# A dilated-attention layer whose weighted sums are queued as filler between the next pair's scores

## The chip, the core and the metric

The kernel runs on one core of a Trainium2 chip. The time is the device time of one execution in microseconds. Matrix products run on TensorE (PE in the profile), elementwise work on VectorE (DVE) and ScalarE (ACT); SyncE (SP) issues the DMAs, and each engine works through its own instructions in a fixed order, waiting on semaphores for the others. What is compared is the median of several executions.

## The reference

A trunk of two layers over 512 tokens of width 1024: layer 0 is a stick-breaking attention, layer 1 the dilated attention that changes here; a feed-forward block and a gated per-layer input follow each. The dilated layer, cut to what matters:

```python
DIL_CONFIGS = ((128, 1), (512, 4), (2048, 16))       # window, dilation; 8 heads of 64 each
def dilated_attention(x, w_in, w_out, cos, sin):
    proj = (x @ w_in).reshape(B, S, G, 3, H, HEAD_DIM)
    for g, (window, dil) in enumerate(DIL_CONFIGS):
        q = apply_partial_rope(proj[:, :, g, 0], cos, sin)
        k = apply_partial_rope(proj[:, :, g, 1], cos, sin)
        v = proj[:, :, g, 2]
        # tokens with the same index modulo dil form a sequence; each attends to a band in it
        o, lse = banded_attention(strided(q), strided(k), strided(v), window // dil)
        ...
    alpha = jax.nn.softmax(jnp.stack(lses, axis=0), axis=0)
    o = jnp.einsum('gbsh,gbshd->bshd', alpha, jnp.stack(outs, axis=0))
    return o.reshape(B, S, H * HEAD_DIM) @ w_out
```

The three groups' softmaxes, weighted by their sums, are one softmax over all keys of the three groups, which is how the kernel computes it.

## The kernel before

Every product is made of three fp32r matmuls (high times high, high times low, low times high), so each operand is split into a rounded part and a rest: ScalarE writes the first (`whi`, `th`, `uh`, `od0h`), VectorE the second (`wlo`, `tl`, `ul`, `od0l`). Weights arrive by DMA and are split the same way in front of their use.

The eight heads are worked through in four pairs. For a pair and a group, `queries(pr, g)` makes the rotated q and k (48 matmuls of 128x512, in two halves), whose outcome VectorE and ScalarE turn into the tiles `dl<pair><group>qa`, `ka`, `la` and so on. `scores` multiplies them (8 matmuls a head) and masks them with a running maximum. `maxima` combines the maxima over groups by transposes, `exps` takes 16 exponentials on ScalarE, in place in the tiles `S`. The sums of a pair are eight steps: `turn` transposes up to four blocks of S on TensorE and splits the result into `th` and `tl`; `apply` multiplies these with the values V (6 or 12 matmuls). Three turns run ahead of the first apply. After four steps of a head, numerators and denominators are combined (`s`, `num`, `den`), and when both heads are through, four reciprocals and a product give the pair's output, split into `od<pair>h` and `od<pair>l`. `out` multiplies these with the output weights, with one step per pair.

Values come first. Those of groups 1 and 2 for the first heads use the normalized input in its order; those of group 0 use copies sorted the other way, `uh` and `ul` (`unsorted`). `sq.columns` and `sq.row` make the row and column factors of the normalization by one-column matmuls; the column factor scales the values, the row factor the rope tables `cs` and `ss`, which every query unit needs.

The order of the work around this is set by a `Filler`: a queue of generators that stands for matmul work with a clock in estimated microseconds. `fill(t)` issues work from the queue for t of its clock, `fill.until(x)` issues until x is done. `due(name)` gives the evacuations on VectorE and ScalarE a place in the order by a due time from the table `TUNE`. In the kernel before, the queue holds all twelve query units and then the second half of the values (`values(1, g)`). The sums are driven from outside: `attend` runs through the steps of one pair (pairs 0 and 1), or of pairs 2 and 3 at once, and calls `tick` after each, which issues queued work and, when a query unit is old enough, the scores of one head (`piece`).

Of the kernel before, what the change touches and what calls it, by code (L numbers as in the profile page):

```python
# [19 lines left out]
P = 128  # L20
T = 512
D = 1024
KT = 8
DFF = 4096
EPS = 1e-6
TUNE = dict(late=4, gap2=1.0, hik=1, lok=0, sqk=1, pieces=4, of=5, og=4, warm=9, wprep=0, s1a=-400, s1b=200, e=25,
            oev=25, qev=-400, hsplit=-200, vev=50, rope=-800, ttr=-100, exps=200, turn=-50, maxi=-50, comb=-100,
            norm=400, res=-400, resk=2, yev=-50, fev=25, gate=0, fin=-50, fe=2.0, ff=0.0, fg=5.0, qlag=5.0, fa=0.57,
            fb=0.32, slope=0.05, lag=8.0, gap=1.2, m0=6.0, m1=5.5, m2=8.0, p0=5.0, p1=2.0, p2=8.0, hp0=6, hp1=30,
            hps=2, blag=1.5, vlag=0.0, fx=5.5, ahead=3, pgap=0.0, vev1=50)  # L30
# [133 lines left out]
def program(tc, ctx, w_dram, x_dram, xs_dram, p_dram, pos_dram, g_dram, c_dram, out_dram):  # L164
# [479 lines left out]
    def dilated(xh, xl, sq, oh, ol, partial, out, prepare):  # L644
        swap = list(range(8, 16)) + list(range(8)) + list(range(16, 32))
        with tc.tile_pool(name="dlw", bufs=1, reuse_waits="tile") as wp:
# [51 lines left out]
                            value_part(g, t0 + 1, ps)  # L698
                        yield 0.72

            def queries(pr, g):
                f = {}

                def evac(m, ps, cs):
                    c, s = norm["rope"]
                    a, b, d = tmp("ra"), tmp("rb"), tmp("rf" + str(m))
                    with due("rope"):
                        dve.stream_shuffle(b, ps, swap)
                        if g:
                            dve.tensor_mul(a, ps, c)  # L710
                            dve.tensor_mul(d, b, s)
                        else:
                            dve.tensor_tensor(sigma(a), cut(ps), cut(c), ALU.mult)
                            dve.tensor_tensor(sigma(d), cut(b), cut(s), ALU.mult)
                        dve.tensor_add(d, d, a)
                    f[m] = d
                    if m == 1:
                        qk[pr, g] = heads_split(f[0], f[1], f"dl{pr}{g}", False, True)

                base = g * 1536 + pr * P  # L720
                yield from linear("w_in_dil", [base, base + 512], xh, xl, evac, bank)

            def scores(S, M, g, h, q, k, kl):

# [58 lines left out]
            def turn(S, order, h, j2):  # L783
# [3 lines left out]
                for j in (2 * j2, 2 * j2 + 1):  # L787
# [6 lines left out]
                    for part in parts:  # L794
                        pe.transpose(ps[:, n:n + P], part, ident)
                        n += P
                fill.clock += 0.45
                th = wp.tile([P, T], F32R, name="th", tag="th", bufs=3)
                tl = wp.tile([P, T], F32R, name="tl", tag="tl", bufs=3)
                with due("turn"):  # L800
# [4 lines left out]
            def apply(pr, order, h, j2, th, tl, out):  # L805
                at = 0
                for j in (2 * j2, 2 * j2 + 1):
                    if order == 0:
                        jobs = [(0, 2 * P if j < 3 else P)]
                    else:  # L810
                        jobs = [(1, P), (2, P)]
                    for g, width in jobs:
                        v = V[g, j]
                        vs, vp = slice(64 * h, 64 * h + P), pr % 2 if g else pr
                        mm3(out[:, j * P:j * P + width], v[:, 0, vp, vs], v[:, 1, vp, vs],
                            th[:, at:at + width], tl[:, at:at + width], j == 0 and g < 2, True)
                        at += width
                fill.clock += 1.3

            def attend(prs, gap, between=None):  # L820
                jobs = [(pr, order, h, j2) for pr in prs for h in range(2) for order in range(2) for j2 in range(2)]
                outs, sums = {}, {}
                ahead = TUNE["ahead"]
                ready, later = [], []
                for j in jobs[:ahead]:
                    ready.append(turn(SS[j[0]], *j[1:]))
                    tick(gap)
                if between is not None:
                    between()

                def divide(pr, num, den):
                    for c in range(4):
                        cs = slice(c * P, (c + 1) * P)
                        i = dve.reciprocal(den[:, cs], den[:, cs])
                        if c == 3:
                            dve.tensor_mul(num, num, den)
                            oh[pr], ol[pr] = split(num, f"od{pr}")
                            later.clear()
                        yield i

                for n, (pr, order, h, j2) in enumerate(jobs):
                    if j2 == 0:
                        outs[order] = wide()
                    apply(pr, order, h, j2, *ready.pop(0), outs[order])
                    if n + ahead < len(jobs):
                        j = jobs[n + ahead]
                        ready.append(turn(SS[j[0]], *j[1:]))
                    if later:
                        after(next(later[0]), norm["turned"])
                    if order == 1 and j2 == 1:  # L850
                        if h == 0:
                            sums[pr] = tmp("num"), tmp("den")
                        num, den = sums[pr]
                        s1 = tmp("s1")
                        hs, ds = HALF[h], HALF[1 - h]
                        with due("comb"):
# [1 line left out]
                            for dst, src in ((den[hs], ds), (num[hs], hs)):  # L858
                                dve.tensor_tensor(cut(dst), sigma(outs[0][src]), cut(s1[src]), ALU.add)
                        if h == 1:  # L860
                            later.append(divide(pr, num, den))
                    tick(gap)
                for d in list(later):
                    run(d)

            vps = {g: [wide(), wide()] for g in (1, 2)}
            for k in range(KT):
                for g in (1, 2):
                    w = W.take("w_in_dil", k, g * 1536 + 1024, 256)
                    for t in range(4):  # L870
                        value_step((xh[k], xl[k]), vps[g][t // 2][:, (t % 2) * 256:(t % 2) * 256 + 256], k, t, *w,
                                   t % 2 == 0)
                if k == 6:
                    norm["col"] = sq.columns(natural_too=True)
                if k == 7:
                    row = sq.row()
            xu = [unsorted(k) for k in range(KT)]
            for g in (1, 2):
                for t in range(4):
                    value_part(g, t, vps[g][t // 2])  # L880
            vps = [bank(), bank(), wide(), wide()]
            for k in range(KT):
                w = W.take("w_in_dil", k, 1024, 512)
                for t in range(4):
# [1 line left out]
            for t in range(4):  # L886
                value_part(0, t, vps[t])
            del xu
            cos, sin = rope_tables()
            rope = [U(n) for n in ("cs", "ss")]  # L890
            dve.tensor_mul(rope[0], cos, row)
            dve.tensor_mul(rope[1], sin, row)
            norm["rope"] = rope
            ones_and_zeros()
            fill = Filler()
            for pr in range(4):
                for g in range(3):
                    fill.add((pr, g), queries(pr, g))
            for g in (1, 2):
                fill.add(("v", g), values(1, g))  # L900
            SS, MM = {}, {}
            pieces = [(pr, g, h) for pr in range(4) for g in range(3) for h in range(2)]

            def piece():
                pr, g, h = pieces.pop(0)
                if pr not in SS:
                    SS[pr], MM[pr] = {}, sp.tile([P, 3, 4, 2], F32, name="M")
                if g < 2:
                    for i2 in range(2):
                        SS[pr][h, g, i2] = U("S")  # L910
                scores(SS[pr], MM[pr], g, h, *(qk.pop((pr, g)) if h else qk[pr, g]))
                fill.clock += 0.87

            def tick(t):
                fill(t)
                if pieces and fill.done.get(pieces[0][:2], 1e9) + TUNE["lag"] <= fill.clock:
                    piece()

            for pr in range(4):
                while pieces and pieces[0][0] == pr:  # L920
                    fill.until(pieces[0][:2], TUNE["lag"])
                    piece()
                    fill(TUNE["pgap"])
                fill(TUNE["m0"])
                N = maxima(MM[pr])
                late = exps(SS[pr], N)[TUNE["late"]:]
                fill(TUNE["m2"])
                if pr < 2:
                    attend([pr], TUNE["gap"])

            def between():
                fill.until(("v", 2))
                for e in late:
                    after(e, norm["last"])
                partial.update({m: bank("out") for m in range(2)})
                fill.add("out", out(partial, (0, 1), range(2)))
                prepare()

            attend([2, 3], TUNE["gap2"], between)
            fill.until("out")  # L940


    def layer(i, h, xh, xl, sq, last):
# [54 lines left out]
        with tc.tile_pool(name=f"ffn{i}", bufs=1, reuse_waits="tile") as fp:  # L998
# [6 lines left out]
            W.pieces = TUNE["pieces"]  # L1005
            if i == 1:
                outs.update({m: wide() for m in range(2, ahead)})
                run(out(outs, range(2, ahead), range(nk - 2)))
                run(out(outs, range(ahead), (nk - 2, nk - 1)))
            run(linear(name, [m * P for m in range(ahead, KT)], oh, ol, lambda m, *a: evac_y(m + ahead, *a),  # L1010
                       banks=wide if i else some(2, bank, wide), nk=nk, halves=True))

# [185 lines left out]
```

## Time and profile before

| quantity | value |
|---|---|
| median of 3 runs | 1470.85 us (1468.16 to 1471.59) |
| profiled execution | 1468.4 us, span 1466.3 us |
| mean granted clock of TensorE | 0.988 |
| TensorE, weight loads | 97%, 82% of the span |
| VectorE, ScalarE, GpSimd | 63%, 47%, 4% |
| the chain that ended last | TensorE 82%, VectorE 10%, ScalarE 5%, issue 2%, DMA 1% |
| the dilated layer up to its output | from 694.2 to 1035.8 us |

The profile is of one execution. Busy time is what an engine spends in its instructions; matmuls are pipelined, and the distance from one start to the next is what one costs in a dense run. In rows of the timeline, square brackets hold the idle time ahead of the instruction and what released it.

### The profile page before, as it was taken

What the parts mean: (1) busy time and instruction counts of PE and PEld (TensorE: products, weight loads), DVE (VectorE), ACT (ScalarE), POOL (GpSimd) and SP (SyncE); (2) the same over time, 40 slices, a digit from 0 to 9 for tenths busy, and PEclk for the clock granted to TensorE, in tenths of its full rate; (3) what the DMA queues carried; (4) which work ended last, traced back from release to release, by engine and by line L of the source; (5) the groups of instructions that cost most, each with busy time, mean ns of one, the idle gap of its engine ahead of it and who ended that gap; (6) DMA issues with size and microseconds to landing.
All of it is one profiled execution on the core that took longest, in us unless ns stands there. A gap on an engine that the chain in (4) does not pass through costs nothing.

```text
span 1466.3 us, 18372 instructions
## 1 busy us (share of the span) xinstructions
PE 1418.8 (97%) x7154; PEld 1198.0 (82%) x7154; DVE 929.6 (63%) x1563; ACT 684.3 (47%) x1042; POOL 56.9 (4%) x33
## 2 busy tenths in 40 slices
PE   9999999999999999999899999898999999999998
PEld 7888888888888888878778787798888888888887
DVE  5888885683353534568759898966783353534476
ACT  4788986543221322355535646644633222222353
POOL 1111110000000000001200000000000000000000
PEclk9999999999999999999899999999999999999999
DMA  5444342333333333223322211220432333333321
GB/s 200 118 113 122 111 117 77 125 96 101 92 96 101 91 97 100 87 87 122 101 64 80 72 46 56 69 70 21 144 98 89 101 93 94 101 89 98 101 74 71
DMA packets 45127, 138.80 MB, mean 95 GB/s; under 512 B 5680, under 2 KB 6448, under 8 KB 45040
## 3 DMA queue, kind: packets, MB, share of 16 engines
q1 hardware_dynamic: 44960, 137.36, 31.5%
q8 instruction: 56, 0.92, 0.3%
q0 software_dynamic: 80, 0.26, 0.1%
q14 instruction: 31, 0.25, 0.1%
HBM read 123.45 MB, written 4.19 MB: 87 GB/s over the span
## 4 chain that ended last, share of the span: by engine, by line
PE 82%; DVE 10%; ACT 5%; issue 2%; DMA 1%; SPq 0%; ACTq 0%; DVEq 0%
PE wb L356 17%; PE wb L358 16%; PE wb L360 16%; PE mmb L356 4%; PE mmb L360 4%; PE mmb L358 3%; DVE wlo L99 2%; PE wb L258 1%; PE wb L259 1%; PE wb L257 1%; ACT S L779 1%; PE mmb L423 1%; PE mmb L425 1%; PE mmb L424 1%; ACT whi L98 1%
## 5 line engine op out<-in xcount | busy, mean ns | idle before, releaser
L98 ACT ACTIVATE whi<-wraw_t 128x1024 fp32r<-128x1024 f32 (+1 forms) x298 | 228.9, 798 | 453.9 <-PE wb L360 345.6
L99 DVE TENSOR_TENSOR wlo<-wraw_t,whi 128x1024 fp32r<-128x1024 f32 (+1 forms) x310 | 276.1, 911 | 234.2 <-ACT whi L98 231.0
L356 PE MATMUL wb<-nh,whi 128*128 128x512 f32 (+1 forms) x594 | 227.3, 385 | 4.4 <-ACT nh L262 4.4
L358 PE MATMUL wb<-nh,wlo 128*128 128x512 f32 (+1 forms) x594 | 226.4, 384 | 0.0
L360 PE MATMUL wb<-nl,whi 128*128 128x512 f32 x576 | 207.6, 391 | 0.4 <-DVE nl L266 0.4
L356 PE MATMUL wb<-fh,whi 128*128 128x512 f32 x496 | 196.5, 396 | 0.0
L360 PE MATMUL wb<-fl,whi 128*128 128x512 f32 x496 | 196.5, 396 | 0.0
L358 PE MATMUL wb<-fh,wlo 128*128 128x512 f32 x496 | 196.4, 396 | 0.0
L356 PEld LDWEIGHTS wb<-nh,whi 128*128 128x128 f32 x594 | 111.7, 188 | 28.7 <-ACT nh L262 7.0
L358 PEld LDWEIGHTS wb<-nh,wlo 128*128 128x128 f32 x594 | 111.7, 188 | 21.7
L360 PEld LDWEIGHTS wb<-nl,whi 128*128 128x128 f32 x576 | 107.8, 188 | 23.3 <-DVE nl L266 1.2
L360 PEld LDWEIGHTS wb<-fl,whi 128*128 128x128 f32 x496 | 93.3, 188 | 22.5
L358 PEld LDWEIGHTS wb<-fh,wlo 128*128 128x128 f32 x496 | 93.3, 188 | 22.4
L356 PEld LDWEIGHTS wb<-fh,whi 128*128 128x128 f32 x496 | 93.3, 188 | 22.4
L356 PE MATMUL mmb<-nh,whi 128*128 128x512 f32 x248 | 101.9, 411 | 3.6 <-DVE V L685 3.6
L360 PE MATMUL mmb<-nl,whi 128*128 128x512 f32 x248 | 98.9, 399 | 0.0
L358 PE MATMUL mmb<-nh,wlo 128*128 128x512 f32 x248 | 98.9, 399 | 0.0
L1088 DVE TENSOR_TENSOR f<-wb,f 128x512 f32<-128x512 f32 (+1 forms) x50 | 33.4, 667 | 73.7 <-PE wb L360 71.4
L1066 ACT ACTIVATE fh<-z 128x512 fp32r<-128x512 f32 x64 | 39.9, 631 | 77.4 <-DVE z L1064 77.4
L1063 DVE TENSOR_TENSOR z<-wb,rrow 128x512 f32<-128x512 f32 x60 | 40.6, 687 | 55.7 <-PE wb L360 55.7
L356 PEld LDWEIGHTS mmb<-nh,whi 128*128 128x128 f32 x248 | 48.0, 194 | 13.1 <-issue 4.0
L289 DVE TENSOR_TENSOR acc<-acc,sq 128x512 f32<-128x512 f32 (+1 forms) x74 | 48.8, 659 | 15.6 <-ACT sq L285 15.0
(1047 smaller groups left out, 2732.2 us busy)
## 6 DMA issues: line engine op xcount, KB each, us to landing
wraw_t<-w SPq DMA_DIRECT2D x219, 512.0 KB, 3.6
x<-x SPq DMA_DIRECT2D x8, 256.0 KB, 6.8
h<-xs SPq DMA_DIRECT2D x8, 256.0 KB, 5.8
spill<-h SPq DMA_DIRECT2D x8, 256.0 KB, 2.8
h<-spill SPq DMA_DIRECT2D x8, 256.0 KB, 5.6
out<-h SPq DMA_DIRECT2D x7, 256.0 KB, 2.0
praw<-p SPq DMA_DIRECT2D x4, 256.0 KB, 4.2
wraw_t<-w SPq DMA_DIRECT2D x4, 128.0 KB, 3.2
```

Of the source, the lines that this page charges most:

```text
L98: self.highs.append(self.nc.scalar.activation(hi[:, c], src[:, c], AF.Copy))
L99: self.lows.append(self.nc.vector.tensor_sub(lo[:, c], src[:, c], hi[:, c].bitcast(F32)))
L257: pe.matmul(ps, ah, bh, start=start, stop=False, skip_group_check=True)
L258: pe.matmul(ps, ah, bl, start=False, stop=False, skip_group_check=True)
L259: pe.matmul(ps, al, bh, start=False, stop=stop, skip_group_check=True)
L289: self.adder.tensor_tensor(self.acc[:, cs], self.acc[:, cs], self.sq[:, cs], ALU.add)
L356: pe.matmul(ps[m][:, cs], wh, xh[k][:, cs], start=(k == 0 and cs is not TWO[1]), stop=False, skip_group_check=True)
L358: pe.matmul(ps[m][:, cs], wl, xh[k][:, cs], start=False, stop=False, skip_group_check=True)
L360: pe.matmul(ps[m], wh, xl[k], start=False, stop=(k == nk - 1), skip_group_check=True)
L1063: dve.tensor_mul(z, ps, norm["row"])
L1066: act.activation(a, z, AF.Copy)
L1088: dve.tensor_add(y[m][:, cs], ps, y[m][:, cs])
```

## The change

The queue now holds the sums too. `attend(pr)` is a generator of one pair whose steps yield 0.45 or 1.75 of the queue's clock, with the division inside. It is queued behind the pair's exponentials: pair 0's sums ahead of the three query units of pair 2, pair 1's ahead of the values of group 1, the queries of pair 3 and the values of group 2, pair 2's alone; pair 3 stays outside, with the output's first three steps issued ahead of it. `piece` makes the scores of both heads at once. The first query unit (pair 0, group 1) is issued in full between the values of groups 1 and 2 and those of group 0, with the row and column factors, rope tables and value evacuations in between. `tick`, `late` and the division spread over other steps go. In `layer`, the output for the first six rows of tiles is issued with three steps and then one, instead of two and two.

```diff
-            def queries(pr, g):
+            def queries(pr, g, banks=bank):
...
-                fill.clock += 0.45        # in turn
...
-                fill.clock += 1.3         # in apply
-
-            def attend(prs, gap, between=None):
...
+            def attend(pr):
+
+                jobs = [(order, h, j2) for h in range(2) for order in range(2) for j2 in range(2)]
+                outs, ready = {}, []
+                for j in jobs[:TUNE["ahead"]]:
+                    ready.append(turn(SS[pr], *j))
+                    yield 0.45
+                for n, (order, h, j2) in enumerate(jobs):
...
                         if h == 1:
-                            later.append(divide(pr, num, den))
-                    tick(gap)
+                            with due("div"):
+                                for c in range(4):
+                                    cs = slice(c * P, (c + 1) * P)
+                                    dve.reciprocal(den[:, cs], den[:, cs])
+                                dve.tensor_mul(num, num, den)
+                                oh[pr], ol[pr] = split(num, f"od{pr}")
+                    yield 1.75
...
+            cos, sin = rope_tables()
...
+            xu = [unsorted(k) for k in range(KT)]
+            for n, _ in enumerate(queries(0, 1, wide)):
+                if n == 2:
                     norm["col"] = sq.columns(natural_too=True)
+                if n == 5:
                     row = sq.row()
+                    norm["rope"] = [U(name) for name in ("cs", "ss")]
+                    dve.tensor_mul(norm["rope"][0], cos, row)
+                    dve.tensor_mul(norm["rope"][1], sin, row)
+                    for g in (1, 2):
+                        for t in range(4):
+                            value_part(g, t, vps[g][t // 2])
...
+            fill.done[0, 1] = -22.0
+            for j in ((0, 2), (0, 0), (1, 0), (1, 1), (1, 2)):
+                fill.add(j, queries(*j))
...
+                for h in range(2):
+                    scores(SS[pr], MM[pr], g, h, *qk[pr, g])
+                    fill.clock += 0.87
...
+                exps(SS[pr], N)
+                order = {0: ["a", (2, 0), (2, 1), (2, 2)], 1: ["a", ("v", 1), (3, 0), (3, 1), (3, 2), ("v", 2)],
+                         2: ["a"], 3: []}[pr]
...
+            fill.until(("a", 2))
+            prepare()
+            partial.update({m: bank("out") for m in range(2)})
+            fill.add("out", out(partial, (0, 1), range(3)))
+            fill(TUNE["m2"])
+            for _ in attend(3):
+                fill(TUNE["gap2"])
             fill.until("out")
...
-                run(out(outs, range(2, ahead), range(nk - 2)))
-                run(out(outs, range(ahead), (nk - 2, nk - 1)))
+                run(out(outs, range(2, ahead), range(nk - 1)))
+                run(out(outs, range(ahead), (nk - 1,)))
```

On ScalarE, at the start of the layer, the order before is this (`V_5870` and `V_5871` are value tiles, `uh` the sorted copies of the input):

```order
L285 ACTIVATE sq<-h_2633 128x512
L665 ACTIVATE uh<-nh 128x4x128 x4
L98 ACTIVATE whi<-wraw_t 128x1024
L665 ACTIVATE uh<-nh 128x4x128 x4
L98 ACTIVATE whi<-wraw_t 128x1024
L684 ACTIVATE V_5870<-wb,rcol 128x2x64
L684 ACTIVATE V_5871<-wb,rcol 128x2x64
```

and of the change this, from the last of the value copies on:

```order
L684 ACTIVATE V_5870<-wb,rcol 128x2x64
L684 ACTIVATE V_5871<-wb,rcol 128x2x64
L98 ACTIVATE whi<-wraw_t 128x1024
L639 ACT_TABLE_LOAD
L639 ACTIVATE cos<-mag 128x512
L640 ACTIVATE sin<-angle 128x512
L665 ACTIVATE uh<-nh 128x4x128 x8
L394 ACTIVATE dl01qa<-rf_6236 64x512
L395 ACTIVATE dl01qb<-rf_6236 64x512
```

The copies `uh` moved from in front of the value copies to behind them, and behind the cosine and sine.

On ScalarE again, at the beginning of the sums of pair 0 (`th` is a turned block, `dl12` the last query unit of pair 1), the change has:

```order
L394 ACTIVATE dl12qa<-rf_7037 64x512
L395 ACTIVATE dl12qb<-rf_7037 64x512
L98 ACTIVATE whi<-wraw_t 128x1024
L800 ACTIVATE th<-wb 128x512
L800 ACTIVATE th<-wb 128x384
L800 ACTIVATE th<-wb 128x512
L398 ACTIVATE dl12ka<-rf_7107 64x512
L399 ACTIVATE dl12kb<-rf_7107 64x512
L400 ACTIVATE dl12ka<-rf_7107 64x512
L401 ACTIVATE dl12kb<-rf_7107 64x512
L800 ACTIVATE th<-wb 128x512 x2
```

where before the exponentials of the same pair led to them:

```order
L779 ACTIVATE S<-S,negmax 128x128
L779 ACTIVATE S<-S,negmax 128x256 x5
L394 ACTIVATE dl11qa<-rf_6883 64x512
L395 ACTIVATE dl11qb<-rf_6883 64x512
L98 ACTIVATE whi<-wraw_t 128x1024
L398 ACTIVATE dl11ka<-rf_6948 64x512
L399 ACTIVATE dl11kb<-rf_6948 64x512
L400 ACTIVATE dl11ka<-rf_6948 64x512
L401 ACTIVATE dl11kb<-rf_6948 64x512
L801 ACTIVATE th<-wb 128x512
```

The sums of pair 0 moved by a whole query unit away from the exponentials that they read.

On TensorE, between the sums of pair 2 and those of pair 3, the change has (`out` is a bank of the output product, `od1h` the output of pair 1):

```order
L258 MATMUL out<-od1l,whi 128x512
L259 MATMUL out<-od1h,wlo 128x512
L257 MATMUL out<-od2h,whi 128x512
L258 MATMUL out<-od2l,whi 128x512
L259 MATMUL out<-od2h,wlo 128x512
L257 MATMUL out<-od2h,whi 128x512
L258 MATMUL out<-od2l,whi 128x512
L259 MATMUL out<-od2h,wlo 128x512
L795 MATMUL wb<-consts,S 128x128 x11
L257 MATMUL wb<-th,V_5869 128x256
```

where before the output steps stood among the sums of pair 2, with pairs 0 and 1 alone:

```order
L259 MATMUL wb<-th,V_5869 128x128
L795 MATMUL wb<-consts,S 128x128 x4
L257 MATMUL out<-od1h,whi 128x512
L258 MATMUL out<-od1l,whi 128x512
L259 MATMUL out<-od1h,wlo 128x512
L257 MATMUL out<-od1h,whi 128x512
L258 MATMUL out<-od1l,whi 128x512
L259 MATMUL out<-od1h,wlo 128x512
L257 MATMUL wb<-th,V_5870 128x128
```

The output's step for pair 2 moved from the end of the layer to directly behind the sums of pair 2.

## Rows read from the trace of the kernel before

**Rows 1.** The page, part 1: busy time, share, instructions of each engine.

```profile
PE 1418.8 (97%) x7154; PEld 1198.0 (82%) x7154; DVE 929.6 (63%) x1563; ACT 684.3 (47%) x1042; POOL 56.9 (4%) x33
```

**Rows 2.** Windows: stretch, length, busy time by engine, granted clock, DMA share, GB/s.

```profile
694.00:781.00 87.00, 76.29 (x417) 67.00 (x416) 58.68 (x107) 43.76 (x75) 9.63 (x6) 0.92 0.27 83
...
818.00:937.00 119.00, 111.00 (x636) 95.17 (x635) 102.36 (x236) 70.35 (x119) 0.00 (x0) 0.97 0.18 54
937.00:988.00 51.00, 46.20 (x312) 42.79 (x313) 37.42 (x102) 30.98 (x59) 0.00 (x0) 0.93 0.25 73
988.00:1036.00 48.00, 43.81 (x278) 39.14 (x277) 30.80 (x51) 25.08 (x55) 0.00 (x0) 0.93 0.22 70
```

**Rows 3.** Waits of TensorE, 690 to 1040: in total, times, longest.

```profile
PE wb L795 <- ACT S L779: 5.2, 2, 3.5
PE mmb L671 <- DVE rrow L320: 3.8, 1, 3.8
PE wb L734 <- ACT dl31ka L400: 3.8, 1, 3.8
PE mmb L356 <- DVE V L685: 3.6, 1, 3.6
PE out L257 <- DVE V L685: 1.8, 1, 1.8
PE wb L764 <- DVE m L758: 1.7, 1, 1.7
PE wb L258 <- DVE tl L802: 1.7, 2, 1.0
PE mmb L301 <- DVE acc L289: 1.6, 1, 1.6
PE wb L735 <- ACT dl00la L406: 1.0, 1, 1.0
PE wb L735 <- ACT dl31la L406: 1.0, 1, 1.0
...
PE wb L257 <- ACT th L801: 0.6, 1, 0.6
PE mmb L301 <- DVE natural L297: 0.6, 1, 0.6
```

**Rows 4.** Windows behind two short waits.

```profile
828.00:832.00 4.00, 3.93 (x24) 3.54 (x25) 2.66 (x4) 3.90 (x8) 0.00 (x0) 1.00 0.00 0
876.00:881.00 5.00, 4.95 (x17) 4.01 (x18) 4.87 (x8) 1.22 (x2) 0.00 (x0) 0.66 0.31 84
```

**Rows 5.** Timeline of ScalarE: start, duration, instruction.

```profile
710.59 4.01 ACT L665 ACTIVATE uh<-nh 128x512 fp32r<-128x512 f32 x4
...
739.36 0.62 ACT L640 ACTIVATE sin<-angle 128x512 f32<-128x512 f32 x1
```

**Rows 6.** Timeline of TensorE in a dense run of query matmuls.

```profile
776.20 0.39 PE L358 MATMUL mmb<-nh,wlo 128*128 128x512 f32 x1
776.43 0.39 PE L360 MATMUL mmb<-nl,whi 128*128 128x512 f32 x1
```

**Rows 7.** Timeline at 988, TensorE and VectorE.

```profile
987.89 1.36 PE L795 MATMUL wb<-consts,S 128*128 128x128 f32 x11
...
989.10 1.22 DVE L99 TENSOR_TENSOR wlo<-wraw_t,whi 128x1024 fp32r<-128x1024 f32 x1 [1.44 <-ACT whi L98]
```

**Rows 8.** Timeline of ScalarE: exponentials of pair 0, a value piece.

```profile
822.13 6.29 ACT L779 ACTIVATE S<-S,negmax 128x128 f32<-128x128 f32 x16
...
980.70 0.37 ACT L684 ACTIVATE V<-mmb,rcol 128x128 fp32r<-128x128 f32 x1 [0.42 <-DVE V L685]
```

**Rows 9.** Timeline at the end: ScalarE, VectorE, VectorE.

```profile
1020.89 0.60 ACT L857 ACTIVATE s<-wb 128x512 f32<-128x512 f32 x1 [0.47 <-PE wb L259]
...
1022.95 3.39 DVE L834 RECIPROCAL den<-den 128x128 f32<-128x128 f32 x4
...
1028.92 0.69 DVE L264 TENSOR_TENSOR od3l<-num,od3h 128x512 fp32r<-128x512 f32 x1 [0.70 <-ACT od3h L262]
```

More of the change, by code (lines that the diff above doesn't have):

```diff
@@ L26 @@
 TUNE = dict(late=4, gap2=1.0, hik=1, lok=0, sqk=1, pieces=4, of=5, og=4, warm=9, wprep=0, s1a=-400, s1b=200, e=25,
-            oev=25, qev=-400, hsplit=-200, vev=50, rope=-800, ttr=-100, exps=200, turn=-50, maxi=-50, comb=-100,
+            oev=25, qev=-400, hsplit=-200, vev=50, rope=-800, ttr=-100, exps=200, turn=-50, maxi=-50, comb=-100, div=100,
             norm=400, res=-400, resk=2, yev=-50, fev=25, gate=0, fin=-50, fe=2.0, ff=0.0, fg=5.0, qlag=5.0, fa=0.57,
@@ L720, in queries @@
                 base = g * 1536 + pr * P
-                yield from linear("w_in_dil", [base, base + 512], xh, xl, evac, bank)
+                yield from linear("w_in_dil", [base, base + 512], xh, xl, evac, banks)
             def scores(S, M, g, h, q, k, kl):
@@ L817, in apply @@
                         at += width
-                fill.clock += 1.3
-            def attend(prs, gap, between=None):
[L821 to L826, printed above, removed]
-                    tick(gap)
[L828 to L841, printed above, removed]
+            def attend(pr):
[5 more added lines that the diff above has]
+                for n, (order, h, j2) in enumerate(jobs):
                     if j2 == 0:
@@ L844, in attend @@
                     apply(pr, order, h, j2, *ready.pop(0), outs[order])
[L845 to L849, printed above, removed]
+                    if n + TUNE["ahead"] < len(jobs):
+                        ready.append(turn(SS[pr], *jobs[n + TUNE["ahead"]]))
                     if order == 1 and j2 == 1:
                         if h == 0:
-                            sums[pr] = tmp("num"), tmp("den")
-                        num, den = sums[pr]
+                            num, den = tmp("num"), tmp("den")
                         s1 = tmp("s1")
@@ L860, in attend @@
                         if h == 1:
-                            later.append(divide(pr, num, den))
-                    tick(gap)
-                for d in list(later):
-                    run(d)
+                            with due("div"):
[6 more added lines that the diff above has]
+            cos, sin = rope_tables()
             vps = {g: [wide(), wide()] for g in (1, 2)}
@@ L872, in dilated @@
                                    t % 2 == 0)
-                if k == 6:
+            xu = [unsorted(k) for k in range(KT)]
+            for n, _ in enumerate(queries(0, 1, wide)):
+                if n == 2:
                     norm["col"] = sq.columns(natural_too=True)
-                if k == 7:
+                if n == 5:
                     row = sq.row()
[L877 to L881, printed above, removed]
+                    norm["rope"] = [U(name) for name in ("cs", "ss")]
[4 more added lines that the diff above has]
+                            value_part(g, t, vps[g][t // 2])
+            vps = [wide() for _ in range(4)]
             for k in range(KT):
@@ L888, in dilated @@
             del xu
[L889 to L893, printed above, removed]
             ones_and_zeros()
             fill = Filler()
[L896 to L900, printed above, removed]
+            fill.done[0, 1] = -22.0
@@ L901, in dilated, with piece @@
+            for j in ((0, 2), (0, 0), (1, 0), (1, 1), (1, 2)):
+                fill.add(j, queries(*j))
             SS, MM = {}, {}
-            pieces = [(pr, g, h) for pr in range(4) for g in range(3) for h in range(2)]
-            def piece():
-                pr, g, h = pieces.pop(0)
+            def piece(pr, g):
                 if pr not in SS:
                     SS[pr], MM[pr] = {}, sp.tile([P, 3, 4, 2], F32, name="M")
[L908 to L917, printed above, removed]
+                for n in range(4):
+                    if (n // 2, min(g, 1), n % 2) not in SS[pr]:
+                        SS[pr][n // 2, min(g, 1), n % 2] = U("S")
+                for h in range(2):
+                    scores(SS[pr], MM[pr], g, h, *qk[pr, g])
+                    fill.clock += 0.87
+                qk.pop((pr, g))
@@ L919, in dilated @@
             for pr in range(4):
[L920 to L923, printed above, removed]
+                for g in (0, 1, 2) if pr else (1, 2, 0):
+                    fill.until((pr, g), TUNE["lag"])
+                    piece(pr, g)
                 fill(TUNE["m0"])
                 N = maxima(MM[pr])
-                late = exps(SS[pr], N)[TUNE["late"]:]
-                fill(TUNE["m2"])
@@ L928, in dilated @@
[L928 to L939, printed above, removed]
+                exps(SS[pr], N)
+                order = {0: ["a", (2, 0), (2, 1), (2, 2)], 1: ["a", ("v", 1), (3, 0), (3, 1), (3, 2), ("v", 2)],
+                         2: ["a"], 3: []}[pr]
@@ new lines, in dilated @@
+                for j in order:
+                    if j == "a":
+                        fill.add(("a", pr), attend(pr))
+                    else:
+                        fill.add(j, values(1, j[1]) if j[0] == "v" else queries(*j))
+            fill.until(("a", 2))
[5 more added lines that the diff above has]
+                fill(TUNE["gap2"])
```

## The prediction, made before the changed kernel ran

> **What bounds the kernel now.** I read the page first: TensorE is busy 1418.8 of 1466.3 us, 97% [rows 1], so the time moves only by what TensorE waits for and by what it runs at half clock. The instructions of the two programs differ in the dilated layer alone, which lies between 694 and 1036 us of the profiled execution; the rest is taken as unchanged. Next the table by stretch. Take a stretch's length less its busy time as waiting, and its length times (1 minus its granted clock) as what the clock costs. That gives 10.7 + 7.0 us for 694 to 781 (values, first softmax rows), 8.0 + 3.6 for 818 to 937 (sums of pairs 0 and 1), 4.8 + 3.6 for 937 to 988 and 4.2 + 3.4 for 988 to 1036 (sums of pairs 2 and 3, output) [rows 2]: 45 us is all that this layer has to give. Then the waits of TensorE by releaser, which say what it waited for [rows 3], and two windows behind a wait: behind 1.7 us at 828 the clock stayed at 1.00, behind 1.7 us at 876 it was 0.66 for 5 us, between 1.2 and 2.4 GHz [rows 4]. So a short wait can cost itself, or itself and 5 x 0.34 = 1.7 us more; I call the second part a fall.
>
> **The change part by part.** Both programs issue the same matmuls, so each stretch is reckoned as waits and falls removed against waits and falls added.
>
> **Values, 694 to 781: -5.0 us.** Removed: the waits for acc 1.6, natural 0.6, rrow 3.8 and V 3.6, the wait of the first scores for dl00la 1.0 [rows 3], and the clock's 7.0 [rows 2]; 17.6 in all. They go because 48 query matmuls (48 x 0.23 = 11.0 us by the start-to-start distance [rows 6]) now stand among the column sums and ahead of the unsorted values, where sums and copies were waited for. Added: on ScalarE the eight uh copies, 4.01 us for four, so 1.0 each, were done from 710.59 on, right behind their input [rows 5]. In the new order they stand behind all sixteen V copies, a split, cos and sin. The angle chain on VectorE, which in the kernel before ended among the V pieces just ahead of cos, now stands with the V pieces and two weight splits in front, so that I put its end at 737.2 (a split is 1.2 us [rows 7]); cos and sin, 0.62 each, end at 738.5 [rows 5], the first uh at 739.5. TensorE without its waits (6.0) and the fall behind them (about 1.5) would have reached these values at 722.5 instead of 730, and with the 11 us of queries at 733.5; I take 732.6, since two short column sums now overlap queries. Wait: 739.5 - 732.6 = 6.9. Bounds: 3 us, if the V pieces start as soon as the column sums end and the angles slip between them, and 9 us, if all angles come last. Behind it a fall of 3.0, one behind the column sums of 1.5, and the first scores' wait of about 1.2 (1.0 measured). Together 12.6 against 17.6.
>
> **Scores of pair 0: +0.3 us.** The query units keep their order there but for sixteen more score matmuls in a row; a third of the 1.0 measured for dl00la [rows 3], between 0 and 1.
>
> **Sums of pairs 0 and 1, 818 to 937: +2.8 us.** Removed: the transposes' waits for the exponentials 5.2 (two), the maxima's 1.7 [rows 3], about 1.0 of smaller ones, and the clock's 3.6 [rows 2], because the exponentials (6.29 us for 16 [rows 8]) now run beside other work. Removed too is the switching between some 44 short runs of queries and scores, at about 0.08 us each by my estimate 3.5. In all 15.0. Added: a pair's sums begin as eleven transposes right behind nine query matmuls that end a unit of queries. The transposes take 1.36 [rows 7], and then the first product with tl is due. But on VectorE that unit's shuffle and two products (0.69 a pass, as the last pass of rows 9) and a weight split of 1.22 [rows 7] are ahead of tl, so that it comes 3 x 0.69 + 1.22 + about 0.5 = 3.8 us after the transposes began: 3.8 - 1.4 = 2.4 us of wait. Its bounds are the 1.6 us (th 0.6, then tl 1.0 [rows 3]) of the head at 987.89, where only a weight split and value pieces were in the way, and 3.8. Then th of the fourth group stands behind four copies of 64x512 (1.4 us), and the maxima of the next pair find VectorE at tl (1.35; bounds 0.5 and 1.7, the wait for m [rows 3]). 5.2 for each of the two pairs, with a fall of 1.7 each: 13.8. Four blocks of scores come closer behind their own queries than before; their splits on ScalarE and VectorE are late by about what dl00la cost, 1.0 each [rows 3], bounds 0 and the 3.8 of dl31ka: 4.0. Added 17.8.
>
> **Pair 3's queries and the second half of the values, 937 to 988: +0.5 us.** Removed: the wait for dl31ka 3.8, for dl31la 1.0 and the clock's 3.6 [rows 2, 3]: 8.4. Added: between the value matmuls of group 1 and the queries of pair 3 a bank must come free. The value pieces alternate between ScalarE and VectorE at 0.37 + 0.42 = 0.79 us a step, and on ScalarE they now stand behind the exponentials of pair 2, 6.29 [rows 8], and two weight splits. I take 4.9 with a fall of 1.7; bounds 0 (the exponentials are through before the values end) and 6.3 + 1.1. Scores 1.5 and maxima 0.8 as above. 8.9.
>
> **Sums of pairs 2 and 3 and the output, 988 to 1036: +8.9 us.** Removed: th 0.6 and tl 1.7, the output's wait for V 1.8 [rows 3], the clock's 3.4 [rows 2]: 7.5. Added, in the order of the program: the head of pair 2 at 1.6 plus one value step of 0.79 [rows 8], 2.4; in the middle th behind fourteen exponentials of pair 3 (14/16 of 6.29 = 5.5 us [rows 8], some of it beside six products and the transposes): 2.6, bounds 0 and 4.2, and a fall. Then the third step of the output: its matmuls read od2h and od2l of the pair whose last product has just been issued, and everything behind them on TensorE, the eleven transposes of pair 3 too, stands in the queue. The row s to od3l shows this chain for pair 3: from 1020.89 to 1028.92 + 0.69, 8.7 us, 3.39 of it the four reciprocals [rows 9]; without the weight split in it 7.4. In front of it are only twelve output matmuls, 12 x 0.23 = 2.7: wait 4.7, bounds 4.0 and 6.0, and a fall. In the kernel before, those steps read od0 and od1, and od2 was needed only at the end. The head of pair 3, 1.6 plus two copies for the last stage (0.62 each): 2.9. At the end the chain for od3 is 8.7 against 36 output matmuls, 8.2: 0.5. Sum 2.4 + 2.6 + 4.7 + 2.9 + 0.5 and two falls, 3.4: 16.5; against 7.5 that is +9.0, and I take 8.9.
>
> **Sum.** -5.0 + 0.3 + 2.8 + 0.5 + 8.9 = +7.5. The profiled execution took 1468.4 us (span 1466.3), 2.4 under the median of 1470.85; it gives 1475.9 on its own basis and 1478.4 on the median's. I forecast 1477.
>
> **The rivals.** *Heads as short as the one measured* (faster). If VectorE takes tl of a pair's first group before that query unit's passes, each head of pairs 0 and 1 costs the measured 1.6 and draws no fall, and the exponentials of pair 3 hide behind products: 2 x (5.2 - 1.6 + 1.7) + 2.6 + 1.7 = 14.9 less, 1461. For it: the exponentials' waits and the 8.4 at 951 surely go. Against it: the order of VectorE and ScalarE is fixed, and at 987.89, with a weight split alone in front, 1.6 was lost already. It decides from a first tl less than about 1.6 us after the transposes.
>
> *Short waits without falls* (no change). The new waits are mostly of 1 to 5 us; the one of 1.7 us at 828 left the clock at 1.00 [rows 4]. Without the five falls of 1.7 the sum is +7.5 - 8.5 = -1.0: 1467 to 1470.
>
> *A fall behind every new wait* (much slower). The 1.7 us at 876 brought the clock to 0.66 [rows 4], and the new order has six more waits of 1 us or more (four scores, two maxima) than I gave a fall: 6 x 1.7 = 10.2 more, 1487. The Trainium skill, TensorE: Matmul & The Clock Gate, section HAM oscillation — how this bites in real kernels, speaks for this: bursts of matmuls parted by waits drop to half clock and pay that again behind each wait. The trace agrees at 876 and disagrees at 828.
>
> That the change might not do what it says is left out: the order shows the sums of a pair between the score blocks of the next.
>
> **How the numbers follow.** Forecast 0.42, its own range 1472 to 1482 (the bounds of the value wait, -4 and +2, with those of the exponentials in the last stretch, -2.6 and +1.6). Heads short 0.20, no falls 0.25, falls everywhere 0.13. A measurement of this kernel tells about 0.3% from no change, 4.4 us: same is 1466.4 to 1475.3. Faster takes the heads case and a little of the second: 0.22. Same takes most of the second and the low end of the forecast: 0.27. Slower 0.51. The range leaves a tenth on each side: 1460 to 1486.
>
> **What would show it.** In the changed profile: waits for S, m, rrow and dl31ka gone from TensorE's list (removals); a wait of about 7 for uh or ul ahead of the unsorted values; waits for tl of about 2.4 at the heads of pairs 0 and 1; a wait of about 4.9 for a value piece ahead of pair 3's queries; one of about 4.7 for od2h or od2l. I am wrong if the layer's stretch, 341.6 us from 694.2 to 1035.8, becomes shorter, or if it lengthens while the waits for uh, tl and od2 are each under 1 us.

## The result, and the profile after

The changed kernel takes 1479.9 us (median of 8, 1476.6 to 1490.1) against 1471.0; the ratio is 1.0069, 95% interval 1.0046 to 1.0092. It is slower by 0.7%, 3 us above the forecast of 1477 and inside the range. A second set of 6 gave 1479.4 and 1.0075 (1.0051 to 1.0098).

The page of the changed kernel, part 1, and the windows (columns as in [rows 2]) of the same 356 us of both kernels, before first:

```profile
PE 1424.0 (96%) x7154; PEld 1202.3 (81%) x7154; DVE 929.9 (63%) x1563; ACT 684.9 (46%) x1042; POOL 54.8 (4%) x33
```

```profile
690.00:1046.00 356.00, 327.20 (x1899) 285.66 (x1898) 274.89 (x606) 199.23 (x359) 10.63 (x7) 0.95 0.24 73
```

```profile
690.00:1046.00 356.00, 324.22 (x1841) 283.95 (x1841) 268.83 (x592) 191.91 (x339) 7.54 (x6) 0.93 0.22 68
```

The layer's own stretch, before and after:

```profile
694.20:1035.80 341.60, 312.81 (x1818) 273.34 (x1817) 264.14 (x586) 188.78 (x333) 9.63 (x6) 0.95 0.23 70
```

```profile
694.80:1045.40 350.60, 318.82 (x1818) 279.48 (x1817) 264.47 (x586) 188.73 (x333) 7.54 (x6) 0.93 0.22 67
```

The profiled span is 9.5 us longer (1475.8 against 1466.3), and the layer is 9.0 us longer (350.6 against 341.6). TensorE idles 3.0 us more in it (31.8 against 28.8), and its clock is lower: summed over windows of 2 us below 0.95, what half clock takes away is 17.1 us before and 25.6 us after. What is left of the stretch, neither waited nor lost to the clock, is 2.6 us shorter. Old waits were exchanged for new ones of nearly the same sum; the clock pays most of the difference. TensorE's waits in the changed kernel, 690 to 1046, columns as in [rows 3]:

```profile
PE wb L258 <- DVE tl L801: 7.1, 6, 2.7
PE wb L671 <- ACT uh L665: 6.0, 1, 6.0
PE out L257 <- ACT od2h L262: 4.1, 1, 4.1
PE mmb L356 <- DVE V L685: 3.7, 1, 3.7
PE wb L735 <- ACT dl10la L406: 2.1, 1, 2.1
PE wb L750 <- DVE M L747: 1.9, 2, 1.0
PE wb L257 <- ACT th L800: 1.4, 3, 0.6
PE wb L735 <- ACT dl20la L406: 1.2, 1, 1.2
PE wb L735 <- ACT dl00la L406: 1.2, 1, 1.2
...
```

Beside [rows 3]: the waits for S (5.2), rrow, m, dl31ka and acc are gone. In their places stand the four that the prediction named, and the timeline says where:

```profile
737.93 0.80 PE L671 MATMUL wb<-whi,uh 128*128 128x512 f32 x1 [6.00 <-ACT uh L665]
...
837.99 0.58 PE L258 MATMUL wb<-tl,V 128*128 128x256 f32 x1 [2.67 <-DVE tl L801]
...
902.58 0.38 PE L258 MATMUL wb<-tl,V 128*128 128x256 f32 x1 [2.10 <-DVE tl L801]
...
933.40 0.77 PE L356 MATMUL mmb<-nh,whi 128*128 128x512 f32 x1 [3.69 <-DVE V L685]
...
1015.65 0.80 PE L257 MATMUL out<-od2h,whi 128*128 128x512 f32 x1 [4.12 <-ACT od2h L262]
```

The granted clock behind each of these (windows of the changed kernel):

```profile
738.00:742.00 4.00, 4.00 (x11) 3.19 (x12) 3.97 (x9) 4.00 (x5) 0.00 (x0) 0.60 0.05 20
836.00:854.00 18.00, 16.01 (x77) 16.01 (x78) 10.66 (x30) 6.55 (x11) 0.00 (x0) 0.53 0.08 30
902.00:918.00 16.00, 14.05 (x120) 13.46 (x120) 11.41 (x32) 8.06 (x14) 0.00 (x0) 1.00 0.12 34
934.00:940.00 6.00, 6.00 (x17) 4.71 (x16) 0.35 (x1) 0.18 (x1) 0.00 (x0) 0.57 0.13 51
993.00:1005.00 12.00, 12.00 (x69) 11.65 (x69) 4.26 (x10) 9.54 (x24) 0.00 (x0) 0.57 0.24 81
1015.00:1021.00 6.00, 5.35 (x18) 4.33 (x18) 2.44 (x4) 2.73 (x5) 0.00 (x0) 0.50 0.00 0
```

Counted from the end of the wait, half clock lasts 3 to 6 us ahead of dense 512-column matmuls (738, 934). In the sums it lasted 16 us behind the head of pair 0 (the wait of TensorE ahead of the first products of a pair) and about 10 in those of pair 2, yet behind the 2.10 us at the head of pair 1 it did not come at all.

### The profile page after: what moved, and what is told of

It reads as the page before. It is cut to its first block, busy times and chain, and to the rows that moved or that the text cites. A ratio compares the mean times of both kernels' runs of the same rounds, so it can differ in the third digit from the quotient of the medians.

```text
span 1475.8 us, 18357 instructions
## 1 busy us (share of the span) xinstructions
PE 1424.0 (96%) x7154; PEld 1202.3 (81%) x7154; DVE 929.9 (63%) x1563; ACT 684.9 (46%) x1042; POOL 54.8 (4%) x33
## 4 chain that ended last, share of the span: by engine, by line
PE 80%; DVE 13%; ACT 4%; issue 2%; DMA 1%; SPq 0%; POOL 0%; ACTq 0%; DVEq 0%
PE wb L356 16%; PE wb L360 16%; PE wb L358 16%; PE mmb L356 3%; PE mmb L360 3%; PE mmb L358 3%; DVE wlo L99 3%; PE wb L258 1%; PE wb L259 1%; PE wb L257 1%; PE wb L671 1%; PE mmb L423 1%; PE wb L672 1%; PE wb L673 1%; PE mmb L425 1%
## 5 line engine op out<-in xcount | busy, mean ns | idle before, releaser
L356 PE MATMUL wb<-nh,whi 128*128 128x512 f32 (+1 forms) x610 | 233.5, 385 | 4.3 <-ACT nh L262 4.3
L358 PE MATMUL wb<-nh,wlo 128*128 128x512 f32 (+1 forms) x610 | 232.4, 383 | 0.0
L360 PE MATMUL wb<-nl,whi 128*128 128x512 f32 x592 | 213.6, 390 | 0.4 <-DVE nl L266 0.4
L356 PE MATMUL mmb<-nh,whi 128*128 128x512 f32 x232 | 92.4, 398 | 3.7 <-DVE V L685 3.7
L358 PE MATMUL mmb<-nh,wlo 128*128 128x512 f32 x232 | 91.3, 394 | 0.0
L360 PE MATMUL mmb<-nl,whi 128*128 128x512 f32 x232 | 91.3, 394 | 0.0
L306 POOL TENSOR_TENSOR rcol<-ms,half 128x4 f32<-128x4 f32 (+1 forms) x10 | 10.9, 1089 | 1184.8 <-DVE ms L305 1184.8
```

The costliest lines, as they stand in the source:

```text
L356: pe.matmul(ps[m][:, cs], wh, xh[k][:, cs], start=(k == 0 and cs is not TWO[1]), stop=False, skip_group_check=True)
L358: pe.matmul(ps[m][:, cs], wl, xh[k][:, cs], start=False, stop=False, skip_group_check=True)
L360: pe.matmul(ps[m], wh, xl[k], start=False, stop=(k == nk - 1), skip_group_check=True)
```

## The experiments

All times are medians; ratios are to the kernel before, with 95% intervals. The edits are to the changed kernel, and "less" is against the 1479.4 us of its second set.

**The changed kernel again.**

> The changed kernel once more, for a second profile. Theory (the clock falls by chance behind a wait): around 1480 us, ratio to the kernel before 1.007, with the same waits (uh about 6.0, first tl of pairs 0 and 1 about 2.7 and 2.1, od2h about 4.1), but not the same stretches at half clock behind the heads of the sums. Rival (the program fixes the falls): half clock again from 837 to 853 and from 994 to 1004 us, and none behind the head of pair 1 at 902.

1479.4 us, runs from 1476.0 to 1489.0. Up to the sums of pair 2 the waits stand as before (6.0; 2.67 and 2.10; 3.69), but the profiled execution was one of 1489 us, and now half clock came behind both heads. Windows of this second profile:

```profile
840.00:857.00 17.00, 16.29 (x77) 16.29 (x78) 9.38 (x29) 6.53 (x11) 0.00 (x0) 0.50 0.12 32
905.00:921.00 16.00, 15.52 (x74) 15.52 (x75) 9.07 (x28) 6.54 (x11) 0.00 (x0) 0.50 0.11 33
```

The same wait, 2.10 us, cost nothing more in one execution and 8 us in the other. Whether the clock falls behind one of 2 to 3 us differs between executions: what half clock takes from 690 to 1046 is 32.2 us here and 25.6 in the first profile, which is 6.6 of the 11.0 us between the two spans. The rival falls.

The expected 4.1 us for od2h did not come back. The middle of pair 2 ran at full clock this time, and the last stretch has other waits (second profile):

```profile
1011.72 0.38 PE L257 MATMUL wb<-th,V 128*128 128x256 f32 x1 [1.82 <-ACT th L800]
...
1026.71 0.50 PE L257 MATMUL out<-od2h,whi 128*128 128x512 f32 x1 [2.01 <-ACT od2h L262]
```

From the copy `s` of pair 2 to the end of od2h it is 6.8 us in both profiles, but the twelve output matmuls in front ran at half clock here and took 5.1 us instead of 3.0. So the clock changes waits too, and 4.1 is not a constant of the program.

**The output's third step at the end.**

```diff
-            fill.add("out", out(partial, (0, 1), range(3)))
+            fill.add("out", out(partial, (0, 1), range(2)))
...
-                run(out(outs, range(2, ahead), range(nk - 1)))
-                run(out(outs, range(ahead), (nk - 1,)))
+                run(out(outs, range(2, ahead), range(nk - 2)))
+                run(out(outs, range(ahead), (nk - 2, nk - 1)))
```

> The output's third step (od2) goes back to the end of the layer, two steps stay ahead of pair 3. Theory: the wait for od2h (4.1) and the half clock behind it (about 2.5) go, about 6 us less than the changed kernel, 1474 us, ratio 1.003. Rival: the head of pair 3, whose th and tl then stand behind the division of pair 2, takes 3 of it back, 1477 us, ratio 1.005.

1475.6 us, ratio 1.0045 (1.0029 to 1.0062): 3.9 us less, between the two; its interval overlaps that of the changed kernel (1.0051 to 1.0098). The wait for od2h is gone, and the rival is seen too, the head of pair 3 behind pair 2's division (waits from 1012 to 1046 us of this kernel):

```profile
PE wb L258 <- DVE tl L801: 3.0, 2, 2.7
```

**The sorted copies first.**

```diff
+            xu = [unsorted(k) for k in range(KT)]
             cos, sin = rope_tables()
...
-            xu = [unsorted(k) for k in range(KT)]
```

> The sorted copies uh and ul are made ahead of the rope tables in the program, so that they stand ahead of the value copies on ScalarE as in the kernel before. Theory: the wait for uh (6.0) and the half clock behind it (1.7) go, about 7 us less than the changed kernel, 1473 us, ratio 1.002. Rival: the rope tables come later for it, and the first scores wait for the rotated queries instead, so that 4 us or more come back: 1477 us or above, ratio 1.005 or above.

1471.7 us, ratio 1.0008 (0.9990 to 1.0025): 7.7 us less, as the theory said. The wait for uh is gone and no other came for it. On ScalarE the copies stand again between the squares and the value copies; written behind the tables, the same copies were put behind cos and sin. At the head of pair 0 this profile has the same wait of 2.67, but half clock ended about 3 us behind it (window of this kernel), where it had lasted 16:

```profile
829.00:843.00 14.00, 11.06 (x83) 10.69 (x82) 11.42 (x32) 7.40 (x14) 0.00 (x0) 0.88 0.13 39
```

**Dummies in the heads.**

```diff
+                if pr < 3:
+                    spare = wide()
+                    for _ in range(10):
+                        pe.matmul(spare, xh[0][:, :P], xh[0], start=True, stop=True, skip_group_check=True)
                 for n, (order, h, j2) in enumerate(jobs):
```

> Ten matmuls of 128x512 (2.3 us) whose result nobody reads stand between the first transposes and the first products of pairs 0, 1 and 2, in the time in which TensorE waits for th and tl. Theory (the wait is what brings the clock down for 16 and 10 us): no half clock behind these heads, 10 to 13 us less than the changed kernel, 1467 to 1470 us, ratio about 0.999. Rival (the sums bring it down by themselves): the clock falls as before, 1480 us within 2, ratio 1.007.

1474.1 us, ratio 1.0029 (1.0021 to 1.0038): 5.4 us less for work that is thrown away, and runs from 1472.7 to 1476.7, a spread of 4 us instead of 13. Half clock behind the first two heads is gone (windows of this kernel):

```profile
836.00:856.00 20.00, 17.38 (x137) 15.57 (x136) 14.89 (x38) 9.07 (x17) 0.00 (x0) 1.00 0.09 27
900.00:920.00 20.00, 18.64 (x162) 17.97 (x161) 14.25 (x35) 11.64 (x26) 0.00 (x0) 1.00 0.00 1
```

So the idle head starts the fall and not the sums by themselves. The size was over-estimated: about 10 us of half clock still came at 999 to 1009, now behind waits of 1.8 and 1.2 for th and tl in the middle of pair 2, where the exponentials of pair 3 hold ScalarE.

**Needed work in the heads.** The first four steps of the next queued unit stand where the dummies stood.

```diff
-            def attend(pr):
+            def attend(pr, mid=None, at=0):
...
+                    if mid is not None and n == at:
+                        for _ in range(4):
+                            yield next(mid)
...
-                        fill.add(("a", pr), attend(pr))
+                        fill.add(("a", pr), attend(pr, gens[order[1]] if len(order) > 1 else None))
```

> As e4_dummy_heads, but with work that is needed: the next queued unit's first four steps (12 query matmuls of pair 2, 2.7 us; 24 value matmuls, 2.9 us) stand between the first transposes and the first products of pairs 0 and 1. Theory (a filled head keeps the clock): the waits of 2.7 and 2.1 and the half clock behind them go, with nothing paid for dummies: 1471 to 1473 us, ratio 1.001 to 1.002. Rival (the steps only move, and VectorE is late for something else): 1477 us or more, ratio 1.005 or above.

1476.1 us, ratio 1.0040 (1.0028 to 1.0053): between the two, 3.3 us less, nearer the rival. The heads are filled (first tl 0.6) and the spread is 3 us, but new waits have come. One is in the sums of pair 0, for the scores of dl12, with 10 us of half clock behind it; the other is for the q and k of the unit that was moved forward, which are read sooner behind their last matmul (this kernel):

```profile
844.75 0.33 PE L735 MATMUL wb<-dl12la,dl12qa 128*128 128x128 f32 x1 [1.25 <-ACT dl12la L406]
...
879.24 0.47 PE L734 MATMUL wb<-dl20ka,dl20qa 128*128 128x128 f32 x1 [2.74 <-ACT dl20ka L400]
```

```profile
845.00:855.00 10.00, 10.00 (x50) 9.32 (x49) 5.25 (x22) 3.06 (x6) 0.00 (x0) 0.50 0.00 0
```

**Values behind the next queries.**

```diff
-                         1: ["a", ("v", 1), (3, 0), (3, 1), (3, 2), ("v", 2)],
+                         1: ["a", (3, 0), ("v", 1), (3, 1), (3, 2), ("v", 2)],
```

> The queued values of group 1 change places with the first query unit of pair 3, so that no value piece has to leave its bank right behind the exponentials of pair 2. Theory: the wait for V (3.7) and the half clock behind it (2.6) go, 6 us less than the changed kernel, 1474 us, ratio 1.003. Rival (the value pieces hold the bank of the next unit instead): the wait only moves, 1479 us within 2, ratio 1.006.

1474.0 us, ratio 1.0029 (1.0017 to 1.0042): 5.4 us less; the wait for V and the half clock at 934 are gone. The theory holds.

**Two waits undone.**

> The edits of e1_od2_late and e2_uh_early together. Theory (the two waits are independent): 4 and 8 us off the changed kernel's 1479.5, 1468 us, ratio 0.998 to 0.999. Rival (one absorbs the other, or the clock falls elsewhere instead): 1471 us or more, ratio 1.001 or above.

1464.9 us, ratio 0.9970 (0.9954 to 0.9986), 14.5 us less, where the two gave 3.9 and 7.7 alone, 11.6 together; the intervals are too wide to tell 14.5 from 11.6. The rival is out, and the kernel is faster than the kernel before: with these two places as they were, the rest of the change is a gain.

**Everything filled with needed work.** The early uh, the filled heads, the values later, the output's third step at the end, and this:

```diff
+            def early():
+                partial.update({m: bank("out") for m in range(2)})
+                yield from out(partial, (0, 1), range(2))
...
+                        fill.add(("a", pr), attend(pr, gens[order[1]] if len(order) > 1 else early(), 0 if pr < 2 else 4))
```

> Early uh, heads of pairs 0 and 1 filled with query steps, values later, and the output's first two steps inside pair 2's sums where th waits for the exponentials of pair 3; od2 at the end. Theory (all these waits and the half clock behind them are what the change costs): 1460 to 1464 us, ratio about 0.994, faster than the kernel before. Rival (the clock falls in the long runs of sums anyway): 1467 us or more, ratio 0.998 or above.

1463.4 us, ratio 0.9951 (0.9937 to 0.9964). The time is the theory's, its reason only in part: half clock still takes 20.4 us in this profile, behind waits that came instead (dl20ka 2.7, dl30la 2.3, and 3.1 for tl at the head of pair 3). Against the two undone alone, 1464.9, the filled heads and the later values gained 1.5 us, and the intervals overlap.

**Dummies on the two undone, values later.**

> The edits of c1_od2_and_uh and e7_values_later, and the ten dummy matmuls of e4_dummy_heads at the heads of pairs 0 and 1. Theory (the parts add up: c1 measured 1464.9, e7 5 less than the changed kernel, e4 5 less): 1455 to 1459 us, ratio about 0.991, a spread of its runs of 5 us or less. Rival (they overlap, as the heads' half clock is a matter of luck): 1462 us or more, ratio 0.995 or above.

1455.2 us (1454.5 to 1456.6), ratio 0.9905 (0.9892 to 0.9917): the best of all, 1% faster than the kernel before. The parts add up: 14.5, 5.4 and 5.4 make 25.3, and it is 24.2 less. Its windows: the sums of pair 0, and the whole stretch, at 0.98 where the changed kernel has 0.93.

```profile
835.00:855.00 20.00, 18.45 (x126) 16.10 (x125) 15.76 (x38) 11.61 (x27) 0.00 (x0) 1.00 0.00 1
690.00:1046.00 356.00, 338.45 (x1993) 295.67 (x1992) 288.66 (x631) 207.81 (x376) 10.79 (x7) 0.98 0.25 76
```

**Dummies inside the sums.**

```diff
+                    if n == 2 and pr < 2:
+                        spare = wide()
+                        for _ in range(8):
+                            pe.matmul(spare, xh[0][:, :P], xh[0], start=True, stop=True, skip_group_check=True)
```

> The changed kernel with eight matmuls of 128x512 (1.8 us) whose result nobody reads, inside the sums of pairs 0 and 1 behind the second step, after the wait at the head. Theory (what keeps the clock down for 16 us is the alternation of short transposes and products, and a dense run brings it back): half clock behind the head ends within 6 us, time as the changed kernel or up to 4 us less, 1476 to 1480 us. Rival (the length is given by something else): half clock until the last products of the pair as before, and 2 x 1.8 to 3.6 us more, 1483 us or above.

1478.5 us, ratio 1.0060 (1.0047 to 1.0073), runs from 1475.9 to 1480.3. The head's wait of 2.67 stays and the clock falls at 837, but behind the eight dense matmuls at 842.8 it is back (windows of this kernel):

```profile
837.00:845.00 8.00, 6.17 (x26) 5.75 (x27) 6.19 (x10) 4.69 (x8) 0.00 (x0) 0.57 0.23 66
845.00:854.00 9.00, 8.01 (x69) 7.71 (x68) 4.89 (x22) 2.34 (x5) 0.00 (x0) 1.00 0.01 2
```

Against 0.53 up to 854 in the changed kernel. The rival is out by the time and by this window. That the alternation of a few transposes and a few products keeps the clock down is not shown: with early uh, half clock ended soon in the same sums without any dummies. What is seen is half clock for 16 us of such sums at pair 0 in five of six profiles without dummies, though TensorE was busy in them.

## Why the prediction was right

The places were right, and the total, 1477 against 1479.9, was right in good part by luck. In the sum's own terms the waits were to rise by 15.7 us (43.1 added, 27.4 removed), what the clock takes to fall by 4.6 (13.0 added, 17.6 removed), and the switching to give 3.5. In the two profiled executions the waits rose by 3.0, what the clock takes rose by 8.5, and the rest fell by 2.6. The waits came out 13 us under their forecast and the clock 13 us over it, and the two errors cancelled. The layer's stretch became longer, 350.6 against 341.6, so the sign named for being wrong did not appear. By the steps:

**Values.** The wait for uh was forecast at 6.9 and is 6.00; cos ran at 735.70, where the forecast's end of the angle chain (737.2) would have put it at 737.3:

```profile
735.70 0.63 ACT L639 ACTIVATE cos<-mag 128x512 f32<-128x512 f32 x1 [1.28 <-DVE mag L637]
```

The clock behind the wait cost about 2 instead of 3, and the fall behind the column sums did not come. The experiment on uh prices the step at 7.7 us. That the copies moved because the rope tables are written ahead of them is argued and not shown: the experiment put them ahead of the tables and of the first value matmuls at once, and which resource holds them was not tested.

**Sums of pairs 0 and 1.** The first tl came as worked out: shuffle, two products and a weight split ahead of it (VectorE of the changed kernel). With the 0.43 that th takes in front of it, the two heads waited 3.1 and 2.5 against the 2.4 of the forecast, whose bounds count th too.

```profile
834.16 0.72 DVE L708 STREAM_SHUFFLE rb<-mmb 128x512 f32<-128x512 f32 x1
834.91 0.69 DVE L710 TENSOR_TENSOR ra<-mmb,cs 128x512 f32<-128x512 f32 x1
835.52 0.68 DVE L711 TENSOR_TENSOR rf<-rb,ss 128x512 f32<-128x512 f32 x1
836.12 1.22 DVE L99 TENSOR_TENSOR wlo<-wraw_t,whi 128x1024 fp32r<-128x1024 f32 x1
837.25 1.15 DVE L801 TENSOR_TENSOR tl<-wb,th 128x512 fp32r<-128x512 f32 x2
```

The maxima waited 0.93 and 0.99 (1.35 forecast), two of the four score blocks 2.06 and 1.23 (4.0 in all forecast, 3.5 measured with 0.2), and th of the fourth group not at all (1.4 forecast).

**The term that was mis-sized** is "a fall of 1.7 each". It was taken from a fall behind a wait that was followed by dense query matmuls. In the sums one mostly lasts until they end: 16 us at half clock, 8 us lost, when it comes (3 us with early uh). In the profiled execution that is 8 + 0 against the 3.4 of the sum, in the second profile 8 + 8; and about 5 in pair 2 against 1.7. Waits that were put too high hid this error (1.4 twice, the middle of pair 2 and the head of pair 3 below).

**Pair 3's queries.** The wait for a value piece is 3.69 (4.9), the fall cost 2.6 (1.7), the scores 1.6 (1.5). The experiment prices the place at 5.4 us.

**The last stretch.** The wait for od2h is 4.12 (4.7), and 2.01 in the second profile; the head of pair 2 0.57 + 1.16 (2.4 with the clock apart); that of pair 3 0.35 at most instead of 2.9, because the wait for od2 in front of it had given VectorE time; with that wait gone it is 3.0. The wait in the middle of pair 2 (2.6) is only 0.4 where half clock stretched the products over the exponentials, and shows with 1.8 and 1.2 where the clock was whole (second profile).

**The rivals.** *Heads as short as the one measured*: no, 2.67. *Short waits without falls*: right for the head of pair 1 in the first profile, wrong for the other places. *A fall behind every new wait*, 1487: the single executions of 1489 and 1490 come near it in time, but by longer falls and not by more of them; in the profile of 1489 none came behind the maxima or the 1.2 for dl20la. The Trainium skill's section HAM oscillation — how this bites in real kernels (TensorE: Matmul & The Clock Gate), weighed there, describes a kernel whose matmul bursts drop to half clock in the waits of 3 to 5 us between them. The traces agree at the heads of pair 0 (2.67 us, half clock in every profile with an idle head) and disagree at the head of pair 1 in the first profile (2.10 us, clock 1.00). With dummies at work in both heads half clock stayed away.

## What to carry to other kernels

When work is moved to fill one engine's waits, list what each moved block needs at its own start: here the old waits did go, and the heads of the moved blocks, a copy put behind a table and an output step put too close to its division cost more than they, with the half clock behind them. Price a wait of TensorE by what follows it: in this kernel half clock cost 2 to 3 us ahead of dense matmuls and up to 8 ahead of short alternating ones. Do not take a total that comes out right as proof of its terms. A wait of 2 to 3 us that could not be removed was worth filling here, even with matmuls that nobody reads. Judge such a change by several profiles: the first one showed one of two falls.

## What the runs showed of the hardware

Equal waits of the same program drew half clock in one execution and not in another (2.10 us at the head of pair 1: clock 1.00 in one profile, 0.50 for 16 us in the other). Over the seven profiles with idle heads, the 2.67 us at pair 0 drew half clock each time, for 3 to 16 us behind the wait, and the 2.10 us at pair 1 twice. The kernels with idle heads and no dummies scatter by 10 to 15 us (1465.4 to 1480.2 with early uh, 1469.8 to 1483.0 with od2 late), those with filled heads by 2 to 5 us. Twenty dummy matmuls, about 4.5 us of work, are part of the fastest kernel of the study.
